# A two-layer hybrid decoder step: residual steps on two tiles in place, the norm's sums inside a weight unit, and the state-space parameters one instruction at a time

## The chip, the core and the metric

The kernel runs on one core of a Trainium2 chip. The metric is the device time of one execution in microseconds (us); times are given as the median of several runs. A core has a matrix engine (TensorE, PE in the rows; its weight loads are PEld), a vector engine (VectorE, DVE), an activation engine (ScalarE, ACT), a general engine (GpSimd, POOL) and a sync engine (SyncE, SP), which here only issues transfers. Each works through its own list of instructions in order and waits for others by semaphores.

## The reference

One step of a decoder trunk with d_model 2048 over 304 token columns (16 meta tokens, 256 of the prompt, 8 x 4 being decoded). Layer 0 mixes by differential attention and a convolution module, layer 1 by a state-space model; both have a SwiGLU feed-forward part (ffn) of width 5632. What the change touches is what lies between these parts:

```python
def rms_norm(x, g):
    xf = x.astype(jnp.float32)
    y = xf * lax.rsqrt(jnp.mean(xf * xf, axis=-1, keepdims=True) + EPS)
    return (y * g.astype(jnp.float32)).astype(x.dtype)

    for l in range(DEPTH):
        h = rms_norm(x, prm['norm_mix_pre'][l])
        ...
        x = x + rms_norm(m, prm['norm_mix_post'][l])
        h = rms_norm(x, prm['norm_ffn_pre'][l])
        f = swiglu(h, prm['w_ffn_gate'][l], prm['w_ffn_up'][l], prm['w_ffn_down'][l])
        x = x + rms_norm(f, prm['norm_ffn_post'][l])

    # in the state-space mixer, per state, from small parameters:
    dt = jnp.exp(prm['ssm_log_dt'][o].astype(f32))[:, None]
    abar = jnp.exp(lam_c * dt)
    coef = (abar - 1.0) / lam_c
```

So each join of two parts needs two norms in a row: the sum of squares of the part's output, `x` updated, and the sum of squares of the new `x`.

## The kernel before

**Tiling.** `x` lies as 16 tiles of 128 features by 304 columns (288 in layer 1's second half, where the meta tokens are dropped, `c0` = 16). Every fp32 product is made of three matmuls (`mm3`, lines 207 to 209) of a high and a low part: weights are split into `whi` (a cast on ACT, line 151) and `wlo` (a subtraction on DVE, line 152), activations into `hh` (ACT, line 438) and `hl` (DVE, line 439). A weight unit is 128 x 1024: four k-tiles by 256 output columns, so 8 steps of three matmuls, 24 in all. Units are loaded by SP into a ring of 9 and split up to 3 ahead into 2 pairs of `whi`/`wlo` (`PAIRS`), with one or two more in the ffn stages. `run` (its loop over `self.jobs` starts at line 167) emits everything in program order; that order is also the order on each engine. There is no planner, except for the side work below.

**Entry of a part.** `start_parts` (line 387) makes the six parts of an entry, and `panels` (line 268) interleaves them with the units of the first three output panels. Row i of an entry is the i-th unit of each of these three panels, 72 matmuls for the four k-tiles 4i to 4i+3. `part(0)` waits for the norm's factor `pb` (in PSUM, tile `nrm`) and makes tiles 0 to 3. Behind the units of a row come the next row's tiles, two at a time (`half`): for each tile, `post_tile` (line 427) multiplies `acc` by `pb` into `py` (line 431) and adds `py` times the gain to `x` (line 432), and `pre_tile` makes `hh` and `hl`. With the second half of a row come the squares of the four tiles of the row before (`sq`): a square on ACT into `sqt`, an add on DVE into `sqa` (line 361). In the last row `seed` stands between the first unit and the second: `sumsq_cols` (line 368) makes six or three one-column matmuls with `ones` (line 375) and then, in eleven instructions on three columns, the reciprocal root on DVE (`rstd_cols`, lines 316 to 329). `rs` and the panels' ends stand between the second unit and the third: three transposes on PE (`bcast_cols`, line 337) spread the root over all partitions, ACT copies it to `rs`, and `flush` emits what hangs on finished panels: in an ffn the middle of SwiGLU (lines 505 to 510). Layer 0's own entry has no `post_tile`, as no part precedes it.

**Finishing a part.** The last matmuls of a part hand each of the 16 output tiles to `down_tile`, `o_tile` or `out_tile`, which write it to `acc` and call `sumsq_add` for its square; the 16th square goes to PE in its own tile.

**Tail.** `last_post` (line 446) does the last norm: a product on DVE into one of three `py` buffers for each of 16 tiles; then for ten tiles a gain on ACT (454) and an add on POOL (455), and for six an add with the gain on DVE (457); and one output transfer of 144 KB per tile from SP.

**Side work.** During ffn 0, `Pre` (line 1456) computes the state-space parameters of layer 1. `tick` is called at every second k-step, four times in a unit, and emits at most one piece from the list, once its predecessor is 3.0 (parameters) or 1.8 (blocks) us of planned matmul time old. The parameters are 11 pieces, each of up to 23 instructions on tiles of 64 to 320 columns (`params1` to `zeros`); behind them come 16 rounds of ten kinds of pieces each.

## Time and profile before

| | us |
|---|---|
| median of three runs (2967.59, 2973.47, 2976.68) | 2973.47 |
| the profiled execution | 2969.4 |
| its span | 2967.6 |
| PE busy in the span | 2811.0 (95%) |
| DVE busy | 1821.5 (61%) |
| ACT busy | 1248.4 (42%) |
| POOL busy | 184.1 (6%) |

The span is what the profiler's records cover; the execution's time is 1.8 us longer. An engine is busy while at least one of its instructions is in flight, so PE's 95% doesn't mean that its matmuls follow each other without a gap: the starts of the matmuls tell that. In the timelines a row is one instruction, or several of a kind in a row (x), with its start, its length, and in brackets how long the engine stood idle ahead of it and who ended that. The part of an idle time that a previous matmul's record covers is not counted in the brackets.

### The profile page before, as it was taken

What the parts mean: (1) busy time and instruction counts of PE and PEld (TensorE: products, weight loads), DVE (VectorE), ACT (ScalarE), POOL (GpSimd) and SP (SyncE); (2) the same over time, 40 slices, a digit from 0 to 9 for tenths busy, and PEclk for the clock granted to TensorE, in tenths of its full rate; (3) what the DMA queues carried; (4) which work ended last, traced back from release to release, by engine and by line L of the source; (5) the groups of instructions that cost most, each with busy time, mean ns of one, the idle gap of its engine ahead of it and who ended that gap; (6) DMA issues with size and microseconds to landing.
All of it is one profiled execution on the core that took longest, in us unless ns stands there. A gap on an engine that the chain in (4) does not pass through costs nothing.

```text
span 2967.6 us, 56665 instructions
## 1 busy us (share of the span) xinstructions
PE 2811.0 (95%) x22603; PEld 2658.3 (90%) x22603; DVE 1821.5 (61%) x3222; ACT 1248.4 (42%) x2227; POOL 184.1 (6%) x420
## 2 busy tenths in 40 slices
PE   8998898799899999999999888899899999999997
PEld 8776676488899999999999888899799999999997
DVE  6444498636886667776645778655754454554555
ACT  4334223334435554444533466443444333333333
POOL 1011100000001111111100012000000000000001
PEclk9999999799999999999999999999899999999998
DMA  6887897984356666666654568555355555555552
GB/s 228 317 292 287 322 339 296 357 303 134 121 168 209 213 199 207 194 202 208 204 160 152 199 216 265 172 199 168 109 176 160 172 164 167 169 158 173 169 156 83
DMA packets 169994, 607.42 MB, mean 205 GB/s; under 512 B 20305, under 2 KB 22770, under 8 KB 169474
## 3 DMA queue, kind: packets, MB, share of 16 engines
q1 hardware_dynamic: 147602, 522.58, 52.8%
q0 software_dynamic: 20688, 76.24, 7.5%
q10 hardware_dynamic: 1440, 4.98, 0.4%
q8 instruction: 177, 2.90, 0.4%
q14 instruction: 87, 0.71, 0.1%
HBM read 563.63 MB, written 40.10 MB: 203 GB/s over the span
## 4 chain that ended last, share of the span: by engine, by line
PE 70%; DVE 10%; ACT 4%; DMA 2%; issue 2%; POOL 0%; SPq 0%; POOLq 0%; DVEq 0%; ACTq 0%
PE pan L207 22%; PE pan L208 22%; PE pan L209 22%; DVE wlo L152 3%; ACT whi L151 1%; DVE oc L1264 1%; PE pvp L1128 1%; DVE odd L1264 1%; DMA ring<-in_w_gu 1%; ACT U L1843 1%; DMA ring<-in_cv 1%; DVE x L432 1%; PE yps L1914 1%; PE sps L1852 1%; DVE sqa L361 1%
## 5 line engine op out<-in xcount | busy, mean ns | idle before, releaser
L152 DVE TENSOR_TENSOR wlo<-ring,whi 128x1024 fp32r<-128x1024 f32 (+1 forms) x734 | 880.7, 1201 | 857.9 <-ACT whi L151 838.3
L207 PE MATMUL pan<-hh,whi 128*128 128x304 f32 (+1 forms) x3936 | 1209.2, 307 | 22.6 <-ACT hh L438 15.3
L209 PE MATMUL pan<-hh,wlo 128*128 128x304 f32 (+1 forms) x3936 | 1193.4, 303 | 24.0 <-DVE wlo L152 23.8
L208 PE MATMUL pan<-hl,whi 128*128 128x304 f32 (+1 forms) x3936 | 1193.3, 303 | 6.7 <-DVE hl L439 3.5
L151 ACT CAST whi<-ring 128x1024 fp32r<-128x1024 f32 (+1 forms) x734 | 752.3, 1028 | 916.2 <-PE pan L208 658.0
L207 PEld LDWEIGHTS pan<-hh,whi 128*128 128x128 f32 x3936 | 753.0, 191 | 56.3 <-issue 22.2
L209 PEld LDWEIGHTS pan<-hh,wlo 128*128 128x128 f32 x3936 | 753.2, 191 | 33.9 <-DVE wlo L152 30.9
L208 PEld LDWEIGHTS pan<-hl,whi 128*128 128x128 f32 x3936 | 752.7, 191 | 9.0 <-DVE hl L439 8.7
L207 PE MATMUL pan<-mh,whi 128*128 128x304 f32 (+1 forms) x1408 | 422.3, 300 | 0.0
L209 PE MATMUL pan<-mh,wlo 128*128 128x304 f32 (+1 forms) x1408 | 419.9, 298 | 0.0
L208 PE MATMUL pan<-ml,whi 128*128 128x304 f32 (+1 forms) x1408 | 419.7, 298 | 0.0
L207 PEld LDWEIGHTS pan<-mh,whi 128*128 128x128 f32 x1408 | 265.1, 188 | 1.2 <-issue 1.2
L209 PEld LDWEIGHTS pan<-mh,wlo 128*128 128x128 f32 x1408 | 265.1, 188 | 0.0
L208 PEld LDWEIGHTS pan<-ml,whi 128*128 128x128 f32 x1408 | 264.9, 188 | 0.0
L507 ACT ACTIVATE g<-g 128x304 f32<-128x304 f32 (+1 forms) x88 | 39.7, 452 | 169.3 <-DVE g L505 169.2
L1128 PE MATMUL pvp<-ring,xs 128*32 128x256 f32 x1024 | 75.5, 418 | 14.8 <-DMA ring<-in_cv 8.7
L361 DVE TENSOR_TENSOR sqa<-sqa,sqt 128x304 f32<-128x304 f32 (+1 forms) x123 | 57.6, 469 | 36.1 <-ACT sqt L357 31.1
L354 POOL MEMSET sqt<- 128x80 f32 x4 | 0.7, 164 | 1206.2 <-DVE sqa L361 1206.2
L510 DVE TENSOR_TENSOR ml<-u,mh 128x304 fp32r<-128x304 f32 (+1 forms) x88 | 41.1, 467 | 44.6 <-ACT mh L509 44.6
L1128 PEld LDWEIGHTS pvp<-ring,xs 128*32 128x32 f32 x1024 | 28.6, 116 | 43.8 <-DMA ring<-in_cv 13.2
L1051 PE MATMUL psS<-ring,qb 128*32 128x256 f32 x1024 | 67.5, 390 | 0.0
L1843 ACT COPY U<-u 32x76 f32<-32x76 f32 x256 | 64.5, 252 | 3.4
(400 smaller groups left out, 2850.4 us busy)
## 6 DMA issues: line engine op xcount, KB each, us to landing
ring<-in_w_gu SPq DMA_DIRECT2D x352, 512.0 KB, 3.5
ring<-in_ck SPq DMA_DIRECT2D x128, 512.0 KB, 5.8
ring<-in_cv SPq DMA_DIRECT2D x128, 512.0 KB, 5.9
ring<-in_w_dn SPq DMA_DIRECT2D x128, 512.0 KB, 3.5
ring<-in_w_qkv SPq DMA_DIRECT2D x48, 512.0 KB, 6.9
ring<-in_w_dn SPq DMA_DIRECT2D x64, 384.0 KB, 3.4
ring<-in_w_cc SPq DMA_DIRECT2D x32, 512.0 KB, 6.6
ring<-in_w_oe SPq DMA_DIRECT2D x32, 512.0 KB, 6.5
```

The lines of the kernel that those rows point to most:

```text
L151: nc.scalar.copy(j.hi[:, :n], j.raw[:, :n])
L152: nc.vector.tensor_tensor(j.lo[:, :n], j.raw[:, :n], j.hi[:, :n].bitcast(F32), op=ALU.subtract)
L207: mm(out, wh, xh, start=start, stop=False)
L208: mm(out, wh, xl, start=False, stop=False)
L209: mm(out, wl, xh, start=False, stop=stop)
L361: nc.vector.tensor_tensor(self.sq[:, c0:T], self.sq[:, c0:T], t[:, c0:T], op=ALU.add)
L507: nc.scalar.activation(g, g, AF.Silu)
L510: nc.vector.tensor_tensor(self.ml[:, m, c0:], u, self.mh[:, m, c0:].bitcast(F32), op=ALU.subtract)
L1051: nc.tensor.matmul(self.psS[32 * j:32 * j + 32, hf * 256:hf * 256 + 256], self.qb[:, g, 4 * hf + j, 32 * b4:32 * b4 + 32], rv[:, :, 4 * hf ...
L1128: nc.tensor.matmul(self.pv[32 * n:32 * n + 32, :256], self.S[:, n // 2, pg * P + 32 * b4:pg * P + 32 * b4 + 32], raw[:, n * 256:n * 256 + ...
L1264: nc.vector.scalar_tensor_tensor(c, src, w, c, op0=ALU.mult, op1=ALU.add)
L1843: nc.scalar.copy(U2[32 * j:32 * j + 32, q], uv[32 * q:32 * q + 32, j])
```

## The change

- **Gain.** `scale_acc` multiplies each tile of `acc` by the post-norm's gain on ACT as soon as the tile and its square are there, for all 64 tiles of the four parts. The joins then have plain products and sums: `acc` times `pb` in place, and `x` plus `acc`.
- **Two tiles.** `post_pair` does this for two tiles in one instruction (608 or 576 columns) in rows 1 to 3 of an entry; the first four tiles are still done one by one.
- **Squares.** In an entry, ACT squares two tiles of `x` at a time into columns of `acc` that are no longer needed, and DVE adds them to `acc`'s first two tiles, one such add for each step instead of four single ones behind every second step. The seed has six matmuls instead of three.
- **Mid-unit.** A unit has a table `mid` of what is emitted behind its z-th step. `seed` stands behind the fourth step of the last row's second unit; `rs`, the ends and the flush stand behind the third step of the last row's third unit. This holds for all four entries, layer 0's own too.
- **Tail.** `last_post` has eight products of two tiles on DVE; POOL adds tiles 0 to 5 one by one, and DVE adds tiles 6 to 15 in five pairs; 11 output transfers instead of 16; ACT has no part in it.
- **Parameters.** `Later` records each instruction of the parameter functions, and each becomes a piece of its own that may be emitted at any tick after its predecessor.

```diff
@@ run
-                for f in (g for fs in zip(*steps) for g in fs):
+                for z, f in enumerate(g for fs in zip(*steps) for g in fs):
                     f()
+                    for g in j.mid.get(z, ()):
+                        g()
@@ panels
-                    jobs += us[0:1] + [Job(start[4])] + us[1:2] + [Job(start[5])]
-                    jobs += [e for _, e in first[:2]] + [Job(self.flush)] + us[2:]
+                    us[1].mid[3] = [start[4]]
+                    us[2].mid[2] = [start[5]] + [e.use for _, e in first[:2]] + [self.flush]
+                    jobs += us
@@ start_parts
+        def square(k):
+
+            if k == 0 and c0:
+                self.nc.gpsimd.memset(self.acc[:, 0:3, :c0], 0.0)
+            self.nc.scalar.activation(self.acc[:, k:k + 2, c0:], self.x[:, k:k + 2, c0:], AF.Square)
+
+        def add(k):
+
+            if k:
+                s = self.acc[:, 0:2, c0:]
+                self.nc.vector.tensor_tensor(s, s, self.acc[:, k:k + 2, c0:], op=ALU.add)
+
+        def pair(k):
+
+            square(k - 2)
+            self.post_pair(k, c0)
+            self.pre_high(k, gpre, c0)
+            self.pre_high(k + 1, gpre, c0)
+            add(k - 2)
+            self.pre_low(k, gpre, c0)
+            self.pre_low(k + 1, gpre, c0)
...
-            return (lambda: half(4 * i), lambda: (half(4 * i + 2), sq(i - 1)), (lambda: sq(3)) if i == 3 else None)
-        return [lambda: part(0), steps(1), steps(2), steps(3), seed, rs]
...
+            k = 4 * i
+            if gpost is None:
+                return (lambda: half(k), lambda: (half(k + 2), sq(i - 1)), (lambda: sq(3)) if i == 3 else None)
+
+            def s2():
+                square(14)
+                add(14)
+            return lambda: (i == 1 and square(0), pair(k)), lambda: pair(k + 2), s2 if i == 3 else None
+        return [part, steps(1), steps(2), steps(3), seed, rs]
+
+    def post_pair(self, k, c0):
+
+        a, x = self.acc[:, k:k + 2, c0:], self.x[:, k:k + 2, c0:]
+        pb = self.pb[:, c0:T].unsqueeze(1).to_broadcast([P, 2, T - c0])
+        self.nc.vector.tensor_tensor(a, a, pb, op=ALU.mult)
+        self.nc.vector.tensor_tensor(x, x, a, op=ALU.add)
+
+    def scale_acc(self, k, gpost, c0=0):
+        a = self.acc[:, k, c0:]
+        self.nc.scalar.activation(a, a, AF.Copy, scale=self.gains[:, gpost, k:k + 1])
@@ last_post
-        def add(k, y):
-            g, xk = self.gains[:, gpost, k:k + 1], self.x[:, k, c0:]
-            if k % 8 in (0, 2, 3, 5, 6):
-                nc.scalar.activation(y, y, AF.Copy, scale=g)
-                nc.gpsimd.tensor_tensor(xk, xk, y, op=ALU.add)
-            else:
-                nc.vector.scalar_tensor_tensor(xk, y, g, xk, op0=ALU.mult, op1=ALU.add)
-            nc.sync.dma_start(self.outs["y"][:, k, c0:], xk)
...
+        for k in range(0, KT, 2):
+            a = self.acc[:, k:k + 2, c0:]
+            pb = self.pb[:, c0:T].unsqueeze(1).to_broadcast([P, 2, T - c0])
+            nc.vector.tensor_tensor(a, a, pb, op=ALU.mult)
+            for i in (k, k + 1):
+                if i < 6:
+                    x = self.x[:, i, c0:]
+                    nc.gpsimd.tensor_tensor(x, x, self.acc[:, i, c0:], op=ALU.add)
+                    out(i, i + 1)
+        for k in range(6, KT, 2):
+            x = self.x[:, k:k + 2, c0:]
+            nc.vector.tensor_tensor(x, x, self.acc[:, k:k + 2, c0:], op=ALU.add)
+            out(k, k + 2)
@@ ffn, down_tile (o_tile and out_tile likewise)
                     self.sumsq_add(a, c0, i == KT - 1)
+                    self.scale_acc(i, 4 * l + 3, c0)
@@ Pre.open
-        for f in (lambda: self.params1(0), lambda: self.params1(1), lambda: self.step_modulus(0),
-                  lambda: self.step_modulus(1), self.params2, self.turns, self.powers, self.coef,
-                  lambda: self.q_rows(0), lambda: self.q_rows(2), self.zeros):
-            p = Piece(f, (p, 3.0 if p.fn else self.LATE))
...
+        ops = []
+        self.nc = LaterNC(k.nc, ops)
+        for f in (self.params1, self.step_modulus, self.params2, self.turns, self.powers, self.coef, self.q_rows, self.zeros):
+            f()
+        self.nc = k.nc
+        for z, f in enumerate(ops):
+            p = Piece(f, (p, 0.0 if z else self.LATE))
```

The order of instructions at the three places the prediction speaks of. On DVE at ffn 0's entry, two steps in a row, before (line 431 is the product, 432 the sum, 439 `hl`, 361 the squares' add, 152 a weight's low half):

```order
L431 TENSOR_TENSOR py<-acc,nrm 128x304
L432 SCALAR_TENSOR_TENSOR x<-py,gains,x 128x304
L431 TENSOR_TENSOR py<-acc,nrm 128x304
L432 SCALAR_TENSOR_TENSOR x<-py,gains,x 128x304
L439 SCALAR_TENSOR_TENSOR hl<-x,gains,hh 128x304 x2
L361 TENSOR_TENSOR sqa<-sqa,sqt 128x304 x4
L152 TENSOR_TENSOR wlo_90<-ring,whi_89 128x1024
L152 TENSOR_TENSOR wlo_9043<-ring,whi_9042 128x1024
L431 TENSOR_TENSOR py<-acc,nrm 128x304
L432 SCALAR_TENSOR_TENSOR x<-py,gains,x 128x304
L431 TENSOR_TENSOR py<-acc,nrm 128x304
L432 SCALAR_TENSOR_TENSOR x<-py,gains,x 128x304
```

and after (464 and 465 are the pair's product and sum, 425 the squares' add, 480 `hl`):

```order
L464 TENSOR_TENSOR acc<-acc,nrm 128x608
L465 TENSOR_TENSOR x<-x,acc 128x608
L425 TENSOR_TENSOR acc<-acc 128x608
L480 SCALAR_TENSOR_TENSOR hl<-x,gains,hh 128x304 x2
L152 TENSOR_TENSOR wlo_90<-ring,whi_89 128x1024
L152 TENSOR_TENSOR wlo_9059<-ring,whi_9058 128x1024
L464 TENSOR_TENSOR acc<-acc,nrm 128x608
L465 TENSOR_TENSOR x<-x,acc 128x608
L425 TENSOR_TENSOR acc<-acc 128x608
L480 SCALAR_TENSOR_TENSOR hl<-x,gains,hh 128x304 x2
L152 TENSOR_TENSOR wlo_88<-ring,whi_87 128x1024
```

Four instructions on two tiles became two, the four squares' adds behind every second step became one add in front of `hl` in every step, and the splits keep their places behind the steps.

On PE in the last row of ffn 0's entry, before; `nrm<-ones` are the seed's matmuls, `whi_87` and `whi_89` belong to the row's first and second unit:

```order
L207 MATMUL pan<-hh,whi_87 128x304
L208 MATMUL pan<-hl,whi_87 128x304
L209 MATMUL pan<-hh,wlo_88 128x304
L375 MATMUL nrm<-ones,sqa 128x1 x3
L207 MATMUL pan<-hh,whi_89 128x304
L208 MATMUL pan<-hl,whi_89 128x304
L209 MATMUL pan<-hh,wlo_90 128x304
```

and after:

```order
L209 MATMUL pan<-hh,whi_89 128x304
L210 MATMUL pan<-hl,whi_89 128x304
L211 MATMUL pan<-hh,wlo_90 128x304
L379 MATMUL nrm<-ones,acc 128x1 x6
L209 MATMUL pan<-hh,whi_89 128x304
L210 MATMUL pan<-hl,whi_89 128x304
L211 MATMUL pan<-hh,wlo_90 128x304
```

The seed moved back by twelve matmuls, from the seam between two units into the middle of the second, and reads `acc` instead of `sqa`.

On DVE in the parameter chain of ffn 0, the end of `powers` before (lines 1560 to 1565 are one complex product, 1583 the negated copy):

```order
L1560 TENSOR_TENSOR ptmp<-swr 128x64
L1561 TENSOR_TENSOR ptmp<-swi 128x64
L1562 TENSOR_TENSOR swr<-ptmp 128x64
L1563 TENSOR_TENSOR ptmp<-swr,swi 128x64
L1564 TENSOR_TENSOR ptmp<-swi,swr 128x64
L1565 TENSOR_TENSOR swi<-ptmp 128x64
L1583 TENSOR_SCALAR swn<-swi 128x320
L152 TENSOR_TENSOR wlo_9043<-ring,whi_9042 128x1024
```

and after, where each instruction is emitted through line 1492 (`Later`):

```order
L1492 TENSOR_TENSOR swi<-ptmp 128x64
L1492 TENSOR_TENSOR ptmp<-swr 128x64
L1492 TENSOR_TENSOR ptmp<-swi 128x64
L1492 TENSOR_TENSOR swr<-ptmp 128x64
L152 TENSOR_TENSOR wlo_88<-ring,whi_87 128x1024
L1492 TENSOR_TENSOR ptmp<-swr,swi 128x64
L1492 TENSOR_TENSOR ptmp<-swi,swr 128x64
L1492 TENSOR_TENSOR swi<-ptmp 128x64
L1492 TENSOR_SCALAR swn<-swi 128x320
L152 TENSOR_TENSOR wlo_90<-ring,whi_89 128x1024
```

Before, the whole piece (21 instructions and two fills of single columns) stood between two splits; after, at most four instructions of it stand between any two.

## Rows read from the trace of the kernel before

**Rows 1.** The page, part 1: each engine's busy time, share of the span, instructions.

```profile
PE 2811.0 (95%) x22603; PEld 2658.3 (90%) x22603; DVE 1821.5 (61%) x3222; ACT 1248.4 (42%) x2227; POOL 184.1 (6%) x420
```

**Rows 2.** Waits of PE: instruction <- releaser: us in all, times, longest us.

```profile
PE pan L209 <- DVE wlo L152: 24.5, 25, 5.5
PE pan L207 <- ACT hh L438: 15.3, 7, 7.8
PE nrm L375 <- DVE sqa L361: 12.0, 7, 3.6
```

**Rows 3.** Timeline of PE behind ffn 0's entry: start, us, instruction, shapes.

```profile
770.00 0.30 PE L208 MATMUL pan<-hl,whi 128*128 128x304 f32 x1
...
772.92 0.30 PE L208 MATMUL pan<-hl,whi 128*128 128x304 f32 x1
```

**Rows 4.** Windows: stretch, us, busy us per engine, granted clock, DMA share, GB/s.

```profile
722.00:759.30 37.30, 35.10 (x234) 33.06 (x232) 32.79 (x58) 20.27 (x35) 0.00 (x0) 0.98 0.34 114
759.30:767.60 8.30, 5.04 (x27) 4.83 (x26) 7.03 (x19) 3.18 (x6) 0.00 (x0) 0.79 0.38 126
806.90:849.50 42.60, 35.01 (x225) 33.52 (x224) 38.27 (x104) 12.40 (x16) 0.00 (x0) 0.92 0.34 112
1672.00:1710.00 38.00, 33.84 (x221) 32.34 (x220) 31.68 (x55) 19.87 (x35) 1.60 (x3) 0.95 0.47 165
1722.00:1910.00 188.00, 160.84 (x2469) 152.80 (x2468) 145.83 (x223) 110.79 (x340) 30.88 (x58) 0.96 0.70 232
2098.80:2133.00 34.20, 31.09 (x220) 29.24 (x219) 30.46 (x56) 18.23 (x33) 0.00 (x0) 1.00 0.42 138
2133.00:2144.00 11.00, 7.44 (x36) 7.06 (x34) 7.12 (x19) 3.22 (x6) 0.21 (x2) 0.69 0.42 128
2964.20:2967.60 3.40, 0.00 (x0) 0.00 (x0) 0.00 (x0) 0.00 (x0) 0.00 (x0) 0.50 0.29 103
```

**Rows 5.** Timeline of PE in the parameter chain; idle before and releaser in brackets.

```profile
816.75 0.62 PE L209 MATMUL pan<-hh,wlo 128*128 128x304 f32 x1 [5.46 <-DVE wlo L152]
```

**Rows 6.** Instruction groups of DVE, 712 to 770: count, busy, mean ns, idle before.

```profile
L439 DVE SCALAR_TENSOR_TENSOR hl<-x,gains,hh 128x304 fp32r<-128x304 f32 x16 | 8.5, 532 | 1.2 <-ACT hh L438 1.2
L361 DVE TENSOR_TENSOR sqa<-sqa,sqt 128x304 f32<-128x304 f32 x16 | 7.6, 474 | 1.9 <-ACT sqt L357 0.7
L431 DVE TENSOR_TENSOR py<-acc,nrm 128x304 f32<-128x304 f32 x16 | 7.4, 465 | 0.0
```

**Rows 7.** Timeline of DVE in ffn 0's entry, the start of two groups.

```profile
736.15 1.23 DVE L152 TENSOR_TENSOR wlo<-ring,whi 128x1024 fp32r<-128x1024 f32 x1
737.29 0.46 DVE L431 TENSOR_TENSOR py<-acc,nrm 128x304 f32<-128x304 f32 x1
737.79 0.54 DVE L432 SCALAR_TENSOR_TENSOR x<-py,gains,x 128x304 f32<-128x304 f32 x1
...
749.44 0.47 DVE L431 TENSOR_TENSOR py<-acc,nrm 128x304 f32<-128x304 f32 x1
```

**Rows 8.** Timeline of PE around the seed in ffn 0's entry.

```profile
759.24 0.30 PE L209 MATMUL pan<-hh,wlo 128*128 128x304 f32 x1
762.80 0.80 PE L375 MATMUL nrm<-ones,sqa 128*128 128x1 f32 x6 [3.26 <-DVE sqa L361]
763.46 0.39 PE L207 MATMUL pan<-hh,whi 128*128 128x304 f32 x1
...
768.43 0.56 PE L337 MATMUL nrm<-ident,rc 128*128 128x128 f32 x3
```

**Rows 9.** Timeline of DVE: first and last of the eleven instructions of the root.

```profile
763.70 0.15 DVE L316 TENSOR_SCALAR rc<-nrm 128x3 f32<-128x3 f32 x1
...
765.68 0.16 DVE L329 SCALAR_TENSOR_TENSOR rc<-rc 128x3 f32<-128x3 f32 x1
```

**Rows 10.** Timeline of DVE in the tail.

```profile
2952.34 1.18 DVE L462 TENSOR_TENSOR py<-acc,nrm 128x288 f32<-128x288 f32 x3 [0.77 <-PE nrm L337]
...
2961.54 0.70 DVE L457 SCALAR_TENSOR_TENSOR x<-py,gains,x 128x288 f32<-128x288 f32 x1
```

More of the change, by code (lines that the diff above doesn't have):

```diff
@@ L35, in __init__ @@
         self.raw, self.free, self.phase, self.cover = None, False, None, 0
-        self.joined = None
+        self.joined, self.mid = None, {}
 class Piece:
@@ L366, in sumsq_rstd, with sumsq_cols @@
         return self.sumsq_bcast(*self.sumsq_cols(count))
-    def sumsq_cols(self, count=2048.0):
+    def sumsq_cols(self, count=2048.0, tiles=None):
         ps = self.np.tile([P, 512], F32, name="nrm", bufs=1)
-        last, self.sq_last = self.sq_last, None
-        tiles = [self.sq] if last is None else [self.sq, last]
+        if tiles is None:
+            last, self.sq_last = self.sq_last, None
+            tiles = [self.sq] if last is None else [self.sq, last]
         n = 3 * len(tiles)
@@ L414, in sq @@
                 self.sumsq_add(self.x[:, k, c0:], c0)
-        def seed():
-            self.rstd = self.sumsq_cols()
+        def square(k):
[14 more added lines that the diff above has]
+            self.pre_low(k + 1, gpre, c0)
+        def seed():
+            if gpost is None:
+                self.rstd = self.sumsq_cols()
+                return
+            af = self.acc.rearrange("p k t -> p (k t)")
+            self.rstd = self.sumsq_cols(tiles=[af[:, z * T:z * T + 384] for z in range(2)])
         def rs():
@@ L434, in pre_tile @@
[L434 to L440 removed]
+            k = 4 * i
+            if gpost is None:
+                return (lambda: half(k), lambda: (half(k + 2), sq(i - 1)), (lambda: sq(3)) if i == 3 else None)
@@ new lines, in scale_acc, with post_tile, pre_high @@
+    def scale_acc(self, k, gpost, c0=0):
+        a = self.acc[:, k, c0:]
+        self.nc.scalar.activation(a, a, AF.Copy, scale=self.gains[:, gpost, k:k + 1])
+    def post_tile(self, k, c0):
+        a, x = self.acc[:, k, c0:], self.x[:, k, c0:]
+        self.nc.vector.tensor_tensor(a, a, self.pb[:, c0:T], op=ALU.mult)
+        self.nc.vector.tensor_tensor(x, x, a, op=ALU.add)
+    def pre_high(self, k, gpre, c0):
+        self.nc.scalar.activation(self.hh[:, k, c0:], self.x[:, k, c0:], AF.Copy, scale=self.gains[:, gpre, k:k + 1])
@@ L444, in load_x, with last_post @@
             self.nc.scalar.dma_start(self.x[:, a:b], self.ins["x"][:, a:b])
[L446 removed]
+    def last_post(self, c0):
         nc = self.nc
         self.pb = self.sumsq_rstd()
[L451 to L466 removed]
+        out = lambda a, b: nc.sync.dma_start(self.outs["y"][:, a:b, c0:], self.x[:, a:b, c0:])
+        for k in range(0, KT, 2):
[11 more added lines that the diff above has]
+            out(k, k + 2)
     def ffn(self, l, c0=0, start=None, side=None):
@@ L1366, in o_tile @@
         self.k.sumsq_add(t, 0, i == KT - 1)
+        self.k.scale_acc(i, 1)
     def close(self):
@@ L1439, with __init__, __getattr__ @@
 TWO_PI = 6.283185
+class Later:
+    def __init__(self, eng, out):
+        self.eng, self.out = eng, out
+    def __getattr__(self, name):
+        f = getattr(self.eng, name)
+        return lambda *a, **kw: self.out.append(lambda: f(*a, **kw))
+class LaterNC:
+    def __init__(self, nc, out):
+        self.vector, self.scalar, self.gpsimd = (Later(e, out) for e in (nc.vector, nc.scalar, nc.gpsimd))
 class Pre(Sched):
```

102 lines of the change are left out of this document (36 added, 66 removed).

## Prediction

> **What bounds the kernel now.** I read the busy shares first: TensorE (PE) has a matmul in flight for 95% of the span [rows 1]. With one core and PE as the bound, a change pays only where PE stands still or runs slowly, so the next view is PE's own waits by releaser [rows 2]: its largest are for VectorE (DVE), for the low half of a weight (`wlo`, line 152) and for the sum of squares that the norm's matmuls read (`sqa`, line 361), and for ScalarE (ACT), for the high half of an activation (`hh`, line 438). Then the timeline gives PE's pitch where nothing is late: 21 matmuls of 304 columns from 770.00 to 772.92, 0.139 us each [rows 3]; by columns I take 0.132 us for 288. With that pitch the windows say what a stretch has lost [rows 4]: its length less matmuls times pitch. The reader should see five lossy places, at all of which DVE is busy for most of the stretch.
>
> - Parameter chain, 806.9 to 849.5: 225 x 0.139 = 31.3 of 42.6 us, so 11.3 lost.
> - ffn 0's entry, 722.0 to 759.3: 234 x 0.139 = 32.5 of 37.3, so 4.8 lost. Behind it the seed wait (sums of squares), 759.24 to 762.80 less one pitch: 3.4. Then the granted clock is lower, 0.79 over 759.3 to 767.6: from 763.46 to 768.43 stand 24 matmuls in 4.97 us instead of 3.34, 1.6 more [rows 4, 8].
> - Layer 1's entry, 1672 to 1710: 221 x 0.139 = 30.7 of 38.0, so 7.3 lost, with the granted clock at 0.95: 5% of the 38, less some of it idle, puts about 1.5 of the 7.3 down to the clock.
> - ffn 1's entry, 2098.8 to 2133: 220 x 0.132 = 29.0 of 34.2, so 5.2; then 2133 to 2144 holds some 30 matmuls and six sums, 4.0 + 0.8 of 11.0 us at a granted clock of 0.69, so about 6.
> - Tail: DVE's first product starts at 2952.34 [rows 10], and the span runs 3.4 us past 2964.2, when the last tile is summed [rows 4].
>
> Together some 40 us, 1.3% of the time. Nothing done elsewhere can add to that, as PE has no gaps there.
>
> **Parameter chain, one instruction at a time: -11.** Before, it comes in 11 bursts, each whole between two weight splits; behind the burst in `powers` PE waits 5.46 us for the next `wlo`, until 816.75, and then runs at a lower granted clock (0.92 over the stretch) [rows 4, 5]. After the change a unit of 24 matmuls (3.35 us of PE) has four ticks and thus at most four small instructions. DVE then owes per unit 1.14 for `wlo` (736.15 to the next start [rows 7]), 4 x 0.23 (the eleven three-column instructions from 763.70 to 765.84 take 0.195 each [rows 9]; 64 columns are estimated a little higher) and about 0.8 as the unit's share of SwiGLU's middle, 2.8 in all and under 3.35. So all 11.3 should go; the lower bound is 9, if a 320-column step and a middle meet in one unit. The instructions take longer in all, but what they feed, layer 1's state-space blocks, lies over 1,000 matmul rows ahead of layer 1's entry in the order, so nothing waits for the end of it.
>
> **Entries, two tiles at a time.** A step handles two tiles. Before: product, add, product, add at 0.50, 0.45, 0.50, 0.45 (737.29 to 737.79 is the first [rows 7]), 1.90; two `hl`; and squares summed in bursts of four (16 adds of 0.474 [rows 6]). One group (two steps, three units) has a period of 737.29 to 749.44, 12.15 us [rows 7], against 72 x 0.139 = 10.0 us of PE: that is the loss. After: one product and one add of 608 columns. No row has that size; between 304 columns at 0.465 [rows 6] and 1024 at 1.23 [rows 7] a straight line gives 0.78, bounded by 0.72 (1024 scaled down) and 0.93 (twice 304). The pair costs 0.78 + 0.04 to the add, and 0.69 to the next: 1.52. The squares' add costs 0.71 for two tiles instead of two adds of 0.474 that wait for each other. Two `hl` with their waits for `hh` are 2 x (8.5 + 1.2) / 16 = 1.2 [rows 6]. A group is then 2 x (1.52 + 0.71 + 1.2) + 3 x 1.14 = 10.3, with 0.4 for a wait for a weight, 10.65. The loss per group falls from 2.1 to 0.6, for three groups -3.0 at ffn 0. Against it: the first tile of a pair is finished with the second, about 0.55 later than now, and the group's first matmul waits for that tile. Ends: 0 and -4.8; I take half of the 3.0, **-1.5**, and for ffn 1 by its loss **-1.7**. At layer 1's entry PE waits for weight halves, which DVE and ACT reach sooner: **-2.0** of the 5.8 that the clock leaves, between 0 and -5.
>
> What pays for it is the gain, now multiplied on ACT (one more instruction for each of 64 tiles, at about 0.55) as `acc` is finished. Those stages run at PE's pace with ACT at some 4 of each 16 us; the matmuls of those stages hide it. It would cost something (0.5 a stage) if the scale of tile 14 delayed the last square; that scale is over before DVE hands over tile 15.
>
> A rule against this bears on the pair. The rows show a dependent instruction starting 0.04 us behind the end of the 0.46 us one in front of it, and one that waits for nothing on DVE 0.09 us ahead of the end of the split in front [rows 7]. The Trainium skill, VectorE: DVE Perf Modes, section "The DRAIN you can't avoid", says that a semaphore between chained operations costs nothing extra and that only their number counts. By that, the pair would save 0.25 and not 0.38 us; over 18 pairs in three entries that is 4.5 instead of 6.8 us of DVE time, some 1 us of PE time less. The rows of this trace speak against it.
>
> **The norm's seed in mid-unit: -4.3 and -5.2.** Before, it needs two bursts of four square sums that are queued on DVE around a split, and it is due when a unit ends. After, all but the last pair are already summed; from the last `hl` at 757.2 come one split (1.14) and one add (0.71), 759.1, up to 759.6 with the square on ACT, and it is due four steps into the next unit, 759.4 + 12 x 0.139 = 761.05. So neither the 3.4 nor the 1.6 at ffn 0 should be left; three more one-column matmuls cost 0.66 at most (six records take 0.80 in all [rows 8]): -4.3. ffn 1 likewise: 6.2 less 0.66 would be -5.5; as some matmul records can be missing I take -5.2. Layer 1: the 1.5 at the lower clock goes, the 0.7 comes, and with the -2.0 above that is -2.8.
>
> What is late next is the norm's chain on DVE: due 21 matmuls behind the seed. The split of the coming unit stands ahead of it; it can start only as the unit before the seed frees its pair, at t (the start of that unit): cast 1.04, split 1.22, so t + 2.55. Seed at t + 1.67 + 0.9. Chain 2.14 [rows 9], ready at t + 4.75; the transposes are due at t + 3.35 + 0.7 + 1.25 = t + 5.3. That is 0.5 us to spare, the smallest margin of the change. Behind the chain on DVE is the next split only.
>
> **Tail: -2.0.** Eight products of 576 columns at 0.69 (1024 scaled), then five adds at 0.69: 2952.34 + 9.0 = 2961.3 against 2964.2. The last transfer is two tiles, and five of them follow each other at 0.7 us, so the 3.4 us behind the last tile grow to 4 or 4.3. Ends -3 and -0.5.
>
> Here a single row hints at contention: DVE's add at 2961.54 takes 0.70 [rows 10], against 0.54 for the same kind with 304 columns at the entry [rows 7]. The Trainium skill, SBUF — State Buffer, section "Who interferes with whom", says that a DVE instruction with two SBUF inputs and a GpSimd (POOL) one that reads SBUF shut each other out for a whole instruction. By that the pair adds and POOL's last addition collide once, for about 0.9: -1.1 instead of -2.0.
>
> **Sum.** -11 - 1.5 - 4.3 - 2.8 - 1.7 - 5.2 - 2.0 = -28.5. The profiled execution took 2969.4 us (span 2967.6), 4.1 under the median of 2973.47 of the runs shown. 2969.4 - 28.5 = 2940.9 on its scale; on the median's 2945.
>
> **Rivals.**
>
> 1. The groups do not shrink. The tile a group starts with comes later, and that eats what the period gives: the entries' -1.5, -1.7 and -2.0 vanish, and the first group of each loses 0.5 more. For it: PE's waits for `hh` come to 15.3 us [rows 2], and `hh` is made straight behind the add. Against: DVE's period of 12.15 is longer than PE's 10.0. -22: 2951.
> 2. The groups' losses vanish altogether, as do layer 1's: -3.3, -3.5 and -3.0 more: -38, 2935. For it: 10.65 is near 10.0, and the bounds of a pair reach down.
> 3. The norm's chain is late: the spare 0.5 us is gone by one late split. PE then waits up to 2.3 at each entry in mid-unit and runs 1.6 at a lower clock: 3 x 3.9 = 11.7 given back, 2957.
> 4. The chain, cut up, still holds every split back a little: one instruction per tick, each waiting for the one in front, with ACT and POOL steps among them on which DVE waits in order. Then none of the 11 is gained: 2956.
> 5. Slower: layer 1's mixer. In 1722 to 1910 PE is busy for 160.8 of 188 us [rows 4], so 1.7 us are lost at each of its 16 tiles. How much depends on how DVE's and ACT's steps fall between matmuls, and the flush moved into mid-unit puts all of them in another phase. At 1.8 us more per tile the 28.5 are eaten; from 2.4 us per tile, 38 us, the kernel is slower than before by over 0.3%: at 2.5, 2985. Against it: nothing in that loop's own code changes.
>
> **How the numbers follow.** About 0.3%, 9 us, is what a measurement can tell from no change here. Forecast 0.52 (2938 to 2951), rival 1 0.18, rival 2 0.12, rival 3 0.08, rival 4 0.06, rival 5 with lesser slips of the same kind 0.04. To leave out no more than 2 in 10 I go from rival 2 to just past rivals 3 and 4: 2934 to 2958. Faster by over 0.3% means under 2964.5: all but rival 5 and pairs of rivals 1, 3 and 4 together, 0.90; within 0.3%, 0.07; slower, 0.03.
>
> **What would show it.** In the profile after: PE's waits for `wlo` fall from 24.5 to some 15 us [rows 2], and no wait of over 1 us is left in the chain; the wait for `sqa` of 12.0 keeps only what lies at the three norms between stages. A group's period on DVE is 10.5 to 10.8, with the 608-column operations at 0.72 to 0.85. The transposes of the norm wait for nothing. The last x tile is summed 8.5 to 9.5 us behind the first product. It is wrong if the state-space stretch grows, if waits for `hh` grow by more than `wlo` loses, or if a wait for `rc` comes up at the transposes.

## The result and the profile after

Six runs of each kernel side by side: 2971.43 us before, 2952.84 after (medians), a ratio of 0.9938 with a 95% interval of 0.9923 to 0.9954, so 18.6 us less (13.7 to 22.9 by the interval). The forecast was 28.5 less, in a range of 15.5 to 39.5 less. Of the executions behind the medians below, two far slower ones (15233 us in e6, 3377 us in e7) are left out.

That sum hides two larger ones. The first rows of PE's matmuls for the norms cut the span into stages, and the stages of the two profiled executions differ like this (us; each stage begins with the first sums, or with the transposes, of the norm named):

| stage | before | after | difference | forecast |
|---|---|---|---|---|
| start and layer 0, to the sums behind its output | 712.6 | 716.5 | +3.8 | 0 |
| ffn 0's entry, to the second norm's transposes | 55.8 | 49.5 | -6.3 | -5.8 |
| ffn 0's rest | 889.0 | 875.2 | -13.8 | -11 |
| layer 1's entry | 56.6 | 52.5 | -4.1 | -2.8 |
| layer 1, mixer to output | 372.2 | 388.3 | **+16.1** | 0 |
| ffn 1's entry | 57.3 | 49.9 | -7.4 | -6.9 |
| ffn 1's rest | 804.1 | 802.8 | -1.3 | 0 |
| tail | 19.9 | 17.6 | -2.3 | -2.0 |
| span | 2967.6 | 2952.2 | -15.4 | -28.5 |

After the change the transposes come nine matmuls later; each entry therefore holds 1.25 us that lay in the stage behind it before. Layer 0's 3.8 lie within what that stage differs by from execution to execution: it took 710.4 to 718.0 us in the experiments that leave it as it was before.

The kernel after, PE's waits over the whole span (releaser, us in all, times, longest), the answer to [rows 2]:

```profile
PE sps L1906 <- DVE st L1931: 28.0, 8, 4.5
PE pan L209 <- ACT hh L477: 15.0, 6, 8.0
PE pan L211 <- DVE wlo L152: 14.4, 15, 3.1
...
PE nrm L379 <- DVE sqa L364: 5.1, 5, 2.5
```

`wlo` fell from 24.5 to 14.4 and `sqa` from 12.0 to 5.1, as the prediction wanted. At the top stands one that was 5.1 before: `sps`, the matmuls of layer 1's state-space tiles, waiting for the rotation (`st` is its last instruction) that empties their only PSUM tile. Windows of the kernel after (stretch, us, busy us and instructions of PE, PEld, DVE, ACT, POOL, granted clock, DMA share, GB/s), to be read beside [rows 4]:

```profile
806.00:850.00 44.00, 44.00 (x318) 44.00 (x316) 29.76 (x74) 17.25 (x23) 0.00 (x0) 1.00 0.49 159
1693.70:2081.90 388.20, 353.19 (x3828) 344.42 (x3826) 241.17 (x339) 195.86 (x468) 33.48 (x67) 0.95 0.58 193
```

The chain's stretch is full: 318 matmuls at 0.138 us, and a granted clock of 1.00. The last row is layer 1; the same stretch of the kernel before:

```profile
1714.10:2086.20 372.10, 343.90 (x3837) 335.15 (x3835) 242.80 (x340) 189.04 (x454) 33.43 (x66) 0.98 0.62 203
```

The same work within a few instructions; PE is idle for 35 us instead of 28, and busy for 353 instead of 344 with the granted clock at 0.95 instead of 0.98. By the prediction's own sign ("it is wrong if the state-space stretch grows") its account fails here.

The entry and the seed: DVE's groups from 716 to 768 in the kernel after (against [rows 6]), DVE's timeline of one pair (against [rows 7]), PE's around the seed (against [rows 8]):

```profile
L425 DVE TENSOR_TENSOR acc<-acc 128x608 f32<-128x608 f32 x7 | 5.5, 785 | 0.0
L465 DVE TENSOR_TENSOR x<-x,acc 128x608 f32<-128x608 f32 x6 | 4.8, 794 | 0.2
L464 DVE TENSOR_TENSOR acc<-acc,nrm 128x608 f32<-128x608 f32 x6 | 4.7, 781 | 0.0
```

```profile
734.54 0.78 DVE L464 TENSOR_TENSOR acc<-acc,nrm 128x608 f32<-128x608 f32 x1
735.36 0.79 DVE L465 TENSOR_TENSOR x<-x,acc 128x608 f32<-128x608 f32 x1
736.07 0.78 DVE L425 TENSOR_TENSOR acc<-acc 128x608 f32<-128x608 f32 x1
...
744.04 0.78 DVE L464 TENSOR_TENSOR acc<-acc,nrm 128x608 f32<-128x608 f32 x1
...
754.68 0.78 DVE L464 TENSOR_TENSOR acc<-acc,nrm 128x608 f32<-128x608 f32 x1
```

```profile
761.55 0.30 PE L211 MATMUL pan<-hh,wlo 128*128 128x304 f32 x1
761.69 1.39 PE L379 MATMUL nrm<-ones,acc 128*128 128x1 f32 x12
762.94 0.39 PE L209 MATMUL pan<-hh,whi 128*128 128x304 f32 x1
...
765.95 0.56 PE L340 MATMUL nrm<-ident,rc 128*128 128x128 f32 x3
```

A pair's operations are 0.78 to 0.79 us, the sum 0.82 behind the product on which it depends, the next 0.71 behind that; groups have periods of 9.5 and 10.64, where 10.5 to 10.8 were forecast. Neither the seed nor the transposes wait: the seed starts one pitch behind a matmul, and its sums cost 1.25 where three cost 0.66. The tail on DVE, against [rows 10]:

```profile
2939.51 5.40 DVE L499 TENSOR_TENSOR acc<-acc,nrm 128x576 f32<-128x576 f32 x8 [1.05 <-PE nrm L340]
2944.83 3.43 DVE L507 TENSOR_TENSOR x<-x,acc 128x576 f32<-128x576 f32 x5
```

The last tile is summed 8.75 us behind the first product (11.8 before), and the span ends 3.9 behind that.

### The profile page after: what moved, and what is told of

Same layout as the page of the kernel before. It is cut to its first block, busy times and chain, and to the rows that moved or that the text cites. A ratio compares the mean times of both kernels' runs of the same rounds, so it can differ in the third digit from the quotient of the medians.

```text
span 2952.2 us, 56580 instructions
## 1 busy us (share of the span) xinstructions
PE 2810.6 (95%) x22621; PEld 2664.1 (90%) x22621; DVE 1802.7 (61%) x3153; ACT 1273.8 (43%) x2257; POOL 179.5 (6%) x413
## 4 chain that ended last, share of the span: by engine, by line
PE 73%; DVE 8%; ACT 3%; DMA 2%; issue 1%; SPq 0%; DVEq 0%; ACTq 0%
PE pan L209 23%; PE pan L210 23%; PE pan L211 23%; DVE wlo L152 2%; ACT whi L151 1%; ACT U L1897 1%; DVE oc L1307 1%; DMA ring<-in_w_cc 1%; PE sps L1906 1%; DVE odd L1307 1%; PE pvp L1171 1%; DMA ring<-in_cv 1%; PE yps L1968 1%; DMA ring<-in_w_gu 1%; PE stp L1749 0%
## 5 line engine op out<-in xcount | busy, mean ns | idle before, releaser
L152 DVE TENSOR_TENSOR wlo<-ring,whi 128x1024 fp32r<-128x1024 f32 (+1 forms) x734 | 880.1, 1201 | 890.1 <-ACT whi L151 858.8
L211 PE MATMUL pan<-hh,wlo 128*128 128x304 f32 (+1 forms) x3936 | 1191.1, 303 | 14.6 <-DVE wlo L152 14.4
L151 ACT CAST whi<-ring 128x1024 fp32r<-128x1024 f32 (+1 forms) x734 | 752.8, 1028 | 932.1 <-PE pan L210 681.4
L211 PEld LDWEIGHTS pan<-hh,wlo 128*128 128x128 f32 x3936 | 751.3, 191 | 19.6 <-DVE wlo L152 19.5
L1906 PE MATMUL sps<-U,scr 128*128 128x76 f32 x256 | 40.5, 324 | 28.4 <-DVE st L1931 28.0
L1906 PEld LDWEIGHTS sps<-U,scr 128*128 128x128 f32 x256 | 38.7, 238 | 30.3 <-issue 25.0
```

The costliest lines, as they stand in the source:

```text
L151: nc.scalar.copy(j.hi[:, :n], j.raw[:, :n])
L152: nc.vector.tensor_tensor(j.lo[:, :n], j.raw[:, :n], j.hi[:, :n].bitcast(F32), op=ALU.subtract)
L211: mm(out, wl, xh, start=False, stop=stop)
L1906: nc.tensor.matmul(sp[:, z, q * CH:q * CH + CH], scr[:, z * 512 + q * P:z * 512 + q * P + P], self.st[i]["U2"][:, q], start=True, stop=True)
```

## What held layer 1 up: the rows

A tile of layer 1's mixer goes through a shuffle (16 small copies on ACT, L1897), PE's state matmuls into `sps` (L1906), the rotation on DVE (L1918 to L1931, last into `st`), a scan, the turning back on DVE (L1918 to L1945, last into `H`) and PE's output matmuls into `yps` (L1968). Between these steps come the casts (L151) and splits (L152) of the weights.

The kernel after in layer 1's mixer, DVE (in brackets the idle time ahead of a row, and who ended it):

```profile
1766.79 0.72 DVE L1945 TENSOR_TENSOR H<-rt,rt 128x544 f32<-128x544 f32 x1
1771.60 1.22 DVE L152 TENSOR_TENSOR wlo<-ring,whi 128x1024 fp32r<-128x1024 f32 x1 [4.08 <-ACT whi L151]
1772.74 0.72 DVE L1918 TENSOR_TENSOR rt<-sps,scr 128x544 f32<-128x544 f32 x1
...
1774.77 0.22 DVE L1931 TENSOR_TENSOR st<-sps,scr 128x64 f32<-128x64 f32 x1
```

The same place on ACT and on PE:

```profile
1765.87 4.24 ACT L1897 COPY U<-u 32x76 f32<-32x76 f32 x16
1770.14 0.21 ACT L1946 COPY st<-H 128x8 f32<-128x8 f32 x1
1770.38 0.25 ACT L1947 COPY H<-scr 128x64 f32<-128x64 f32 x1
1770.53 1.04 ACT L151 CAST whi<-ring 128x1024 fp32r<-128x1024 f32 x1
```

```profile
1771.65 0.30 PE L211 MATMUL pan<-hh,wlo 128*128 128x304 f32 x1
1775.24 1.11 PE L1906 MATMUL sps<-U,scr 128*128 128x76 f32 x4 [3.29 <-DVE st L1931]
```

The rotation (from 1772.74) has had its input since 1764.6, when PE's matmuls for it ended. It stands behind a weight's split, for which DVE stands idle 4.08 us, as the cast starts only at 1770.53. By then PE is about to need the rotation: it waits 3.29 us. This comes at every second tile, eight times in all. In the kernel before the split falls on another place of the cycle, ahead of the turning back or behind the rotation, and PE waits 0.65 to 1.96 for `st`, five times:

```profile
1794.29 1.22 DVE L152 TENSOR_TENSOR wlo<-ring,whi 128x1024 fp32r<-128x1024 f32 x1 [1.96 <-ACT whi L151]
...
1796.82 0.72 DVE L1891 TENSOR_TENSOR H<-rt,rt 128x544 f32<-128x544 f32 x1
```

The reason is counting. The mixer's pieces are emitted at ticks, four in a unit, and a tile's cycle is six ticks long; splits are emitted at the seams of units. The flush that marks the first tile stood at a seam, with four ticks to the next; in mid-unit, behind the third step, three are left. One tick more or less decides for all 16 tiles on which side of the rotation the split falls. The order of DVE's rows in the traces agrees: over the stretch eight splits stand straight behind a turning back in the kernel after, one in the kernel before.

## The experiments

All times are medians beside runs of the kernel before on the same chip; "stage" is a row of the table above.

**e1 and e2: the tick alone, in both kernels.**

```diff
-        k.hook, k.fine = self.tick, FINE
+        skip = [1]
+        def tick(t):
+            if skip[0]:
+                skip[0] -= 1
+            else:
+                self.tick(t)
+        k.hook, k.fine = tick, FINE
```

> The changed kernel, with one change: in layer 1's mixer the first call of the side-work clock is ignored, so that all its pieces move back by one tick (six matmuls) against the weight units. Theory (phase): between the changed kernel's norm transposes of layer 1's entry and the first sums of the next norm lie 388.3 us, against 372.2 in the kernel before, because a weight's cast now stands behind the 16 shuffle copies on ACT and its split on DVE ahead of the rotation, at every second tile. One tick gives the old order back: the stretch falls to 370 to 374, PE's waits for the rotation (st) from 28.0 to about 5 us, the time from 2953 to 2937. Rival (load): DVE or ACT simply have more to do there, or the flush comes too late; then the stretch stays at 386 to 390 and the time at 2953.

> The kernel before, with nothing of the change, but the first call of the side-work clock in layer 1's mixer ignored. Theory (phase): the stretch from the transposes of layer 1's entry to the next norm's sums grows from 372 to about 388 us, PE's waits for the rotation (st) from 5.1 to about 28, the time from 2971 to 2987. Rival (load): the tick is lost once, under 1 us, and the time stays at 2971 to 2972.

Measured: e1 2940.58 (0.9902, 0.9888 to 0.9916, of before), layer 1 377.1, the waits for `st` 12.0. e2 2995.12 (1.0082, 1.0060 to 1.0104), layer 1 391.8, `st` 24.6:

```profile
PE sps L1859 <- DVE st L1884: 24.6, 8, 4.4
```

One ignored call, without anything else of the change, makes the kernel before 25 us slower (19.6 by the stage), and 11 of the 16 us come back with it in the changed one. The order on DVE changes with it: e2's is that of the changed kernel, up to one split at the start of the stretch, with the eight splits straight behind a turning back; e1 has none there. The phase is the cause. e1's 377.1 is 3 to 7 above what was expected: two waits of 4.1 and 1.8 us at its first tiles stay.

**e3: the chain alone** (`Later` and the pieces of one instruction, in the kernel before).

> The kernel before, with the parameter chain alone emitted one instruction at a time. My forecast was 11; the changed kernel's trace shows ffn 0 behind its entry shorter by 13.8 us (889.0 to 875.2). If the 13.8 are the chain's, the time falls to 2957 to 2958 and PE's waits for wlo by some 9 us; if part of it came from the entry's other phase, to 2960 or more. Nothing outside ffn 0 moves.

Measured: 2957.32 (0.9963, 0.9951 to 0.9975). ffn 0's rest 877.6 instead of 889.0: -11.4, the forecast's 11.3. Of these, PE's waits for `wlo` give 7.6 (8.3 to 0.7 us from 770 to 1640); over the whole span those waits fall by 6.0, where some 9 were expected. Layer 1's mixer stays at 372.7. The further 2.4 us in the changed kernel are the 1.25 us that moved into the entry and about 1 from the place of the flush (e4 has 877.5 again). In this one execution ffn 0's entry was 2.3 longer and layer 1's 2.8 shorter than before; why, no run shows.

**e4: seed, root and flush at the seams again**, the rest as changed:

```diff
-                    us[1].mid[3] = [start[4]]
-                    us[2].mid[2] = [start[5]] + [e.use for _, e in first[:2]] + [self.flush]
-                    jobs += us
+                    jobs += us[0:1] + [Job(start[4])] + us[1:2] + [Job(start[5])]
+                    jobs += [e for _, e in first[:2]] + [Job(self.flush)] + us[2:]
```

> The changed kernel with the norm's seed, its transposes and the flush put back between whole units, at all four entries; two-tile steps, spread squares, chain and tail stay. Theory: the mixer's phase is the old one again, 372 us instead of 388. At the entries the sums are ready when the seed is due, or up to 0.5 us later, as only one pair's add is behind the last step, so the spread squares and not the place give the seed's 4 to 5 us; the transposes wait some 0.7 us for the root. Time 2937 to 2940. Rival (the place gives it): the seed wait of 3.4 us and the lower clock behind it come back in ffn 0 and ffn 1, 2945 to 2948.

Measured: 2933.81 (0.9881, 0.9863 to 0.9898), clearly faster than before and than the change. Entries 49.8, 51.2 and 49.0, layer 1 373.0, with DVE's order there that of the kernel before. The seed at ffn 0 waits 0.2 us:

```profile
PE nrm L378 <- DVE acc L424: 0.2, 1, 0.2
```

So the place in mid-unit is not what ends the seed's waits, and giving it up repairs the phase.

**e5: mid-unit in the two ffn entries only; e8: the same in the kernel before, with nothing else.**

> The changed kernel with the norm's seed and flush back between whole units at the entries of layers 0 and 1 alone; in both ffn entries they stay in mid-unit. What does the place in mid-unit give by itself, beside the kernel with all four at the seams (2933.8)? By the two traces' stages, with nine matmuls (1.25 us) taken off each entry and put on the stage behind it, mid-unit saves 0.6 to 1.6 us at ffn 0's entry, 1.1 behind it and 0.4 at ffn 1's: 2931 to 2932, with the mixer at 372 to 373. My forecast's reading (the place is worth 4 to 5 us at each) would give 2924 to 2926.

> The kernel before with only the seed and the flush of the two ffn entries moved into mid-unit; squares, steps, chain and tail as before. If the place is what ends the seed's waits (my forecast), each entry gains 4 to 5 us: 2960 to 2962. If it is the spread squares, the sums are as late as before, and only the twelve matmuls between are gained, 1.7 us of the 3.4 at each entry, and part of the 1.6 to 2.2 at the lower clock: 2964 to 2968.

Measured: e5 2934.31 (0.9901, 0.9885 to 0.9917), beside e4's 2933.81 no difference in time; by stages, entry and rest together, 2.5 less in ffn 0 and 0.5 in ffn 1, and 3.4 less in layer 1's mixer (369.6), whose entry is the same in both: that much a stage differs from execution to execution. e8 2963.06 beside 2967.50 (0.9986, 0.9974 to 0.9999), 4.2 us less by the ratio (0.3 to 7.7 by the interval), where the expected times, taken from 2971, meant 9 to 11 and 3 to 7; by stages 1.8 less in ffn 0 and 3.7 in ffn 1. Its seed in ffn 1 still waits 2.0. By these stages the place is worth 1.8 and 3.7 us in the two ffns with bursts, 2.5 and 0.5 with spread squares, not 4 to 5.

**e6: e4 with single tiles** (`post_pair` calls `post_tile` twice).

> The kernel of e4 (all at the seams), with the pair's product and sum made as two products and two sums of one tile each, in the order tile by tile. Theory (DVE sets the pace of the groups): a pair costs DVE 1.90 instead of 1.53 us, a group 0.74 more; nine groups in three entries, of which layer 1's count half: 4 to 6 us more, 2938 to 2940. Rival (the groups only needed the squares spread, and the first tile of a pair comes 0.55 us earlier again): within 1.5 us of 2933.8.

Measured: 2938.87 (0.9905, 0.9887 to 0.9924), overlapping e4's interval, and by chance where it was expected. The stages say the opposite: entries 48.8, 50.1 and 48.0, each 1.0 to 1.1 **less** than e4's. At ffn 0's entry DVE works longer for it (43.9 us against 42.8), and PE is busy for 43.3 us instead of 44.4 at a granted clock of 0.93 instead of 0.90, with the same 5.5 us idle; why, no run shows. An entry that is the same in five kernels (the changed one, e1, e5, e7 and e9 at ffn 0) took 49.5 to 50.5 us, so that 1 us is shown for these two executions only. What stands is that DVE's saving on a pair, forecast as 0.38 us, buys nothing.

**e11: e4 with the squares in bursts**, a row's four tiles together behind the row's second pair.

```diff
-            add(k - 2)
             self.pre_low(k, gpre, c0)
             self.pre_low(k + 1, gpre, c0)
+            if k % 4 == 2:
+                row(k - 6)
```

> The kernel of e4 (all at the seams) with the squares of a row made together behind the row's second pair, as two squares and two adds in a burst, instead of one with each pair. Everything else as in e4. Theory (spreading the squares ends the seed's waits): the sums are one add, 0.71 us, later at the seed, and the first pairs of a row get through sooner. The seed waits 0.5 to 1.5 us at each of three entries: 2935 to 2939, and in the trace 0.5 to 1.5 us more from the first transposes of an entry to its seed. If nothing is lost, it is the halved number of instructions alone (pair-wide squares) that removed the seed's wait.

Measured: 2951.78 (0.9926, 0.9907 to 0.9944). Entries 55.1, 54.0 and 54.9: 5.3, 2.8 and 5.9 more than e4, well above what was expected. In ffn 0's entry:

```profile
PE nrm L378 <- DVE acc L424: 2.3, 1, 2.3
```

The seed waits 2.3 again, and the root's stretch grows from 4.8 to 6.3. Spreading the squares carries most of the entries' gain, 14.0 of the 19.8 us that e4's three are shorter than before. The 5.8 left in e11 lie with what both kernels have: squares two tiles wide, the gain on ACT and the two-tile steps; no run takes the first two out, and none spreads the squares in the kernel before.

**e7, e9, e10, e12: what holds the split.** e7 puts the 16 shuffle copies on POOL, e9 turns the lag of `un` from 1.5 to 0.7, e10 has `RING = 7` and `PAIRS = 3`, e12 is e10 with `AHEAD = 1` and the cast of a unit emitted one unit ahead of its split:

```diff
+            if ns < len(S) and S[ns].raw is not None and getattr(S[ns], "hi", None) is None and self.pairs:
+                cast(S[ns])
```

> The changed kernel with its phase as it is; the 16 shuffle copies of each of layer 1's mixer tiles are on POOL instead of ACT. Theory (the cast of a weight stands behind the shuffle on ACT, its split ahead of the rotation on DVE): with the copies off ACT, DVE's idle times of some 4 us for whi are gone, PE's waits for the rotation fall from 28 to under 8 us, and the stretch from 388 to 375 or less, 2937 to 2940, as long as POOL's copies take no longer than ACT's 4.3 us a tile. If they take twice that, PE waits for the shuffled input instead, and the time says nothing; DVE's idle times still would. Rival (DVE's own load in the new phase): the waits for the rotation stay at 28.

Measured: 2984.52 (1.0064, 1.0044 to 1.0085), layer 1 419.0. POOL needs 5.4 to 8.9 us for a tile's copies, so the first condition failed and PE waits for them instead (32.5 us). DVE's idle time for `whi`, which was to tell the theories apart even so, grew: 56.5 us from 1720 to 1880, against 39.8 in the changed kernel. One row of ACT says what else the cast waits for:

```profile
1785.75 1.05 ACT L151 CAST whi<-ring 128x1024 fp32r<-128x1024 f32 x1 [7.06 <-PE pan L210]
```

With nothing in front of it on ACT, it waits for PE to finish the unit whose pair of tiles it reuses. My first reading, that the shuffle alone holds the cast, fell with that: in the kernel after, ACT's copies run without a gap into the cast at 1770.53, but the last matmul of the unit that frees the pair also starts only at 1770.38.

> The changed kernel with one number changed: the planned lag of the step that turns the scanned states back in layer 1's mixer (un) is 0.7 instead of 1.5. PE's order stays the same to the instruction; on DVE, at every second tile, the rotation comes ahead of the weight's split instead of behind it. New theory, after the POOL run: the cast of that weight waits for PE to finish the unit whose pair it reuses (there, with ACT free, it stood idle 7 us for just that), not for the shuffle; the rotation, whose input has been there for 5 us, stands behind the split, and PE's next state matmuls need the rotation 1.1 us after the unit's end, while cast, split and rotation take 1.05 + 1.14 + 2.3. So the stretch falls from 388 to 370 to 375, waits for st from 28 to under 10, 2935 to 2939. Rival (anything else in the phase, such as the shuffle or the position of PE's blocks): 388 and 2953 stay.

Measured: 2967.99 (0.9988, 0.9973 to 1.0004), layer 1 404.5. The waits for `st` went as expected, and others took their place:

```profile
PE yps L1968 <- issue: 19.3, 13, 5.0
...
PE sps L1906 <- ACT U L1897: 11.5, 16, 2.2
...
PE sps L1906 <- DVE st L1931: 7.0, 2, 4.5
```

Turning back a tick earlier puts ACT's copies of its result ahead of the next shuffle, which then waits for DVE. The waits at `yps` are named "issue", time for which the profile shows no releaser, but all 13 end 0.10 us behind the end of the same instruction, DVE's sum out of `yps` (L1979), which empties that tile's only buffer:

```profile
1796.16 0.50 DVE L1979 SCALAR_TENSOR_TENSOR yt<-u,dcol,yps 128x288 f32<-128x288 f32 x1
1796.76 0.73 PE L1968 MATMUL yps<-H,scr 128*32 128x76 f32 x16 [1.58 <-issue]
```

So here too PE waits for DVE, at another tile. The expectation was right on the wait and wrong on the time.

> The changed kernel with a third pair of split weights throughout (and two ring slots fewer, to make room). DVE's order keeps the split ahead of the rotation, but the split is for a unit later and its pair has been free for a whole unit. Theory: without that wait the order does no harm; the stretch falls from 388 to 372 or less, DVE's idle time for whi in 1720 to 1880 from 40 us to under 10. Rival (the shuffle on ACT holds the cast): the waits at every second tile stay at 3.3 us. What two slots fewer do in layer 0, where transfers are late, is unknown, so the stretch decides and not the time.

Measured: 3018.08 (1.0153, 1.0129 to 1.0177), layer 1 397.7, `st` 27.9. The expectation was mistaken in itself: a pair is taken as soon as it is freed, so the third pair made the split one for a later unit, and its cast still waited for the unit just ended. It tells the theories apart in nothing. Layer 0 took 769.9 us, some 54 more than in the changed kernel, with seven slots and three pairs; no run separates the two.

> The kernel of e10 (three pairs of split weights, seven ring slots) with each weight's cast on ACT emitted one unit ahead of its split on DVE. In layer 1's mixer the orders of PE and DVE are those of the changed kernel to the instruction, the split still stands ahead of the rotation at every second tile, but what it needs has been ready for a unit. e10 only moved the wait: its split was for a later unit, and its cast waited for the unit just ended all the same. Theory (DVE stands idle at that split with the rotation behind it, and PE waits for the rotation): DVE's idle time for whi falls from 40 us (1720 to 1880) to under 10, PE's waits for st from 28 to under 10, and the stretch from 388 (changed kernel) and 398 (e10) to 375 or less. Rival (the order of DVE's work itself is too long for the interval): st stays over 20 and the stretch at 385 or more. The stretch decides, not the time, since seven slots and the other cast order act elsewhere too.

Measured: 3014.93 (1.0143, 1.0124 to 1.0163), with layer 0 at 818.8 us (seven slots, three pairs, less of a lead). The stretch that was to decide went from 397.7 to 344.2 us:

```profile
1797.10:2141.30 344.20, 336.08 (x3827) 329.04 (x3826) 238.19 (x339) 195.15 (x468) 33.51 (x67) 1.00 0.65 219
```

PE's waits for `st` there are 2.1 us, DVE's idle time for `whi` is 3.9 us from 1825 to 1985, and DVE has the split between turning back and rotation without idling:

```profile
1855.99 0.72 DVE L1954 TENSOR_TENSOR H<-rt,rt 128x544 f32<-128x544 f32 x1
1856.63 1.22 DVE L156 TENSOR_TENSOR wlo<-ring,whi 128x1024 fp32r<-128x1024 f32 x1
1857.77 0.72 DVE L1927 TENSOR_TENSOR rt<-sps,scr 128x544 f32<-128x544 f32 x1
```

PE's order is that of the changed kernel, DVE's too up to the place of one later split, DVE's work is the same (238 and 241 us), and 44 us are gone, 28 below the kernel before. So it is the split's wait with the rotation behind it, and not the order as such. Whether the pair or the shuffle holds the cast more, no run separates: e12 takes both away. Its early cast with all nine slots, and in layer 1 alone, was not run.

## Why the prediction was right or wrong

- **Chain, -11: right** in size and mechanism (e3: -11.4), and no wait over 1 us is left in it.
- **Prices on DVE: right.** 0.78 for a pair's operation, 0.82 and 0.71 to the next; the tail's last sum 8.75 us behind the first product. As before the change, a dependent operation starts 0.04 behind the end of the one in front, an independent one 0.08 ahead of it. The Trainium skill, VectorE: DVE Perf Modes, section "The DRAIN you can't avoid", says that the next operation waits until the pipe of the one in front is empty, and that one that is not held starts earlier, which these rows fit. They differ in dependence and not in semaphores alone, so they speak neither for nor against that section's sentence on semaphores, on which the prediction drew.
- **Entries: more than forecast, terms mixed up.** The three entries gained 17.8 us as the stages stand, 21.5 with the 1.25 us taken off each, against 15.5. I put 5.2 of the 15.5 down to two-tile steps and most of the rest to the place in mid-unit. The steps bring nothing (e6), the place brings 2.5 in ffn 0 and 0.5 in ffn 1 (e5), and the spread squares bring 14 in all (e11 against e4). The step that failed is the one that gave the last pair's add as the seed's only wait and then credited the place: its 759.1 to 759.6 was about in time for the seam's 759.4 already, so the place was not needed, and e4's seed, at the seam, waits 0.2 us. The other is "half of the 3.0": nothing of the pair's gain reached PE. The 3.0 itself was a slip, since three groups whose loss falls from 2.1 to 0.6 make 4.5.
- **The norm's chain as the next wait (rival 3): did not come.** The root's last instruction starts at 765.10 and takes 0.16, the transposes start at 765.95: 0.7 us to spare, forecast 0.5.
- **Tail, -2.0: right** (-2.3), with 3.9 us behind the last sum, forecast 4 to 4.3. POOL's six sums end at 2944.9, DVE's begin at 2944.83: they hardly meet, so the forecast collision did not come. The kernel before shows it in its tail: DVE's sums (line 457) take 0.51 to 0.52 us where they begin with POOL idle, and 1.08, 1.06 and 0.70 where one of POOL's sums began first.

```profile
2955.74 1.76 POOL L455 TENSOR_TENSOR x<-x,py 128x288 f32<-128x288 f32 x2 [0.39 <-ACT py L454]
2955.76 1.08 DVE L457 SCALAR_TENSOR_TENSOR x<-py,gains,x 128x288 f32<-128x288 f32 x1
...
2959.62 0.51 DVE L457 SCALAR_TENSOR_TENSOR x<-py,gains,x 128x288 f32<-128x288 f32 x1
```

The trace before thus agrees with the rule of the Trainium skill, SBUF — State Buffer, section "Who interferes with whom", on which the prediction drew; the trace after cannot test it.

- **Layer 1's mixer: the step that failed.** The sum has 0 for it, and the prediction said that nothing done outside its five places could add to the gain, though its own row had PE idle for 27 of 188 us in this stretch [rows 4]. It lost 16.1 us, and e12 shows that it had 28 to give. Rival 5 named place and cause, the flush in another phase, and had 4 in 100; it needed 1.8 us a tile to matter for the sign and measured 1.0. What was missing is that the phase is a fact of the order, not chance: that the split stands between turning back and rotation at every second tile stands in the changed kernel's order before any run. Without these 16 us the time would have been some 2937 (2934 in e4) and the forecast of 2945 too slow by 8 to 11.

The range held since a gain larger than forecast and a loss that was hardly priced cancelled in part, which is no merit of the sum.

## What to carry to other kernels

When code is moved past a clock that paces side work, count the ticks and read in the new order what now stands between two dependent steps: one tick here was worth 11 to 20 us of a stage of 372. An instruction that waits for a buffer costs what is queued behind it; making its input early (e12: 44 us of this stage) paid more here than moving it (e4: 15). And where several edits serve one aim, take them out one by one: of three at the entries one carried the gain, one was worth little, and one bought nothing.

## What the runs showed that I had not expected

- Two engines' order unchanged, and 44 us of 388 gone by a cast made a unit earlier (e12). The granted clock in that stretch is 1.00, against 0.95 in the changed kernel, and PE is busy for 336 us instead of 353 with the same matmuls: 17 of the 44 us lie in its busy time and not in its waits.
- POOL takes 0.41 us for a 32x76 copy (5.4 to 8.9 us for 16 with what runs beside it), ACT 0.27 (4.24 for 16):

```profile
L1897 POOL COPY U<-u 32x76 f32<-32x76 f32 x256 | 104.3, 407 | 24.6 <-DVE u L1868 13.4
```

- A wait that the profile puts down to "issue" can have a plain cause: at `yps`, in the kernels before and after, all five such waits end 0.10 us behind the end of DVE's sum out of that tile, as in e9. One wait of 3.4 to 4.0 us in each of e1, e2 and e4 does not, and what ends those no run here shows.
